# Hybrid decoder step: first norm's scale by quarters, conditioning loads by SyncE, last squares summed singly

## The chip, the cores and the metric

The kernel runs on 1 core of one Trainium2 chip. Its time is the device time of one execution in microseconds (us); a median of several runs is given where there are several. The engines are named as in the profile: PE (TensorE, matrix products), DVE (VectorE), ACT (ScalarE), POOL (GpSimd) and SP (SyncE, which here only issues DMAs). DMAs can be issued from SP, ACT and POOL, each with a queue of its own.

## The reference

One inference step of a decoder trunk with one layer, for a prompt of 256 tokens and 8 sample sequences of 4 tokens (288 columns in all), model width 2048, float32:

```python
mod = silu(c) @ w_ada + b_ada                      # c: one row for the prompt, one for each sample
sh1, sc1, gt1, sh2, sc2, gt2 = split(mod, 6)
xn = rmsnorm(x, g_norm1) * (1.0 + sc1) + sh1
proj = xn @ w_in                                   # LRU, GLA q k v, output gates, mLSTM, merge gates
merged = sum over 3 branches of sigmoid(gate_i) * (y_i @ w_br_i)
x = x + gt1 * (merged @ w_out)
xn = rmsnorm(x, g_norm2) * (1.0 + sc2) + sh2
x = x + gt2 * (square(relu(xn @ w_ff1)) @ w_ff2)
y = rmsnorm(x, g_final)
```

The three branches are an RG-LRU recurrence, gated linear attention and an mLSTM; the last two also read and write states of each sample sequence. Outputs are y and all new states.

## The kernel before

**Layout.** Activations lie with the 2048 features on the partitions, as 16 k-tiles of 128 x 288. Weights stream from memory in tiles of 0.5 MB (128 x 1024: two k-tiles by 512 output columns). Every product is made of float32r parts: a weight tile `raw` is split into `hi` (ACT, L156) and `lo` (DVE, L158), the activation into `xh` and `xl`, and PE adds hi*xh, hi*xl and lo*xh, 24 matmuls a weight tile (`stream`, L148 to L182). Three buffers each of `raw`, `hi` and `lo` let the loads run ahead of PE. SP issues the weight loads in the order in which the program is written (L68, a manual schedule for SP alone); the other engines' instructions are ordered by a scheduler.

**Conditioning.** `w_ada` is 6 kinds (SH1, SC1, GT1, SH2, SC2, GT2) of 2048 x 2048, loaded in units of 1 MB, 16 units a kind, multiplied on PE by silu(c) and put on the partitions by a transpose of `by_feature` (L229). `units()` (L344) lists all of them in order; `load_one()` issues the next unit's load, `visit()` runs the products of all units held, and after the last unit of a kind its `end` writes `mod`. A pattern given to `every()` (L187) says at which weight tile a load (L), a visit (V), a load of x (X) or a part of the norm's squares (N) is placed. `slots` names the buffers that the units take in turn: big tiles by number, `None` for the ring tile `ag`, `"st"` for two half tiles that the sample states also use. `slots["queue"]` is the engine that issues the load: SP at first, POOL from L588 on.

**The first norm.** The scale is applied to x before the first products (`scale`, L476); the row factor 1/rms is not known yet, so the first three blocks (q, k and a part of v, `NPRE = 3`) are multiplied by it afterwards (`by_rstd`, L520) and their shift is added as a product of its own (`shift_product`, L317). For the remaining blocks x is normalised and shifted in place (`normalise`, L498, `shift`, L505). Before, SC1 is made in two halves of 8 k-tiles: eight units and half of x come first, then the three blocks run over k-tiles 0 to 7 and, after the other half, over 8 to 15, added to the first pass on DVE (`add_slot`, L514).

**The sample states.** `mlstm()` (L1208) runs beside the output gate's streams; its state loads (`load`, L1393 to L1396) are issued by POOL into `st` and halves of slot 9, its stores by ACT.

**The end.** The last feed-forward product's evacuation (`ff2`, L1613) adds the residual and the squares of each k-tile (`sumsq`, L387): POOL sums the first 13, DVE adds tiles 13 and 14, and three matmuls with a matrix of ones sum over the partitions; `rstd_of` follows and the output is scaled and stored.

Of the kernel before, what the change touches and what calls it, by code (L numbers as in the profile page):

```python
# [52 lines left out]
def trunk(ctx, tc, io):  # L53
# [200 lines left out]
    def cond_product(name, load, each, cols, stat, finish):  # L254


        acc_ = []

        def products(raw, q):
            if not acc_:  # L260
                acc_.append(pa.tile([P, 512], F32, tag="pa", name=nm("pa")))
            ps = acc_[0]
            w = cols // len(raw)
            for i in range(each):
                k = each * q + i
                for h, r in enumerate(raw):
                    v = r[:, w * i:w * i + w].rearrange("p (m j f) -> p j m f", j=4, f=32)
                    for j in range(4):
                        pace["prod"] = T.matmul(ps[32 * j:32 * j + 32, h * w // 4:(h + 1) * w // 4], stat(k), v[:, j],  # L269
                                                start=k == 0 and h == 0, stop=k == KT - 1, skip_group_check=True)  # L270

        def end():
            hs = range(-(-cols // 1024))
            with tc.high_priority():
                pvs = [by_feature(acc_[0], h, min(256, cols // 4 - 256 * h)) for h in hs]
            for h in hs:
                with tc.high_priority():
                    finish(h, pvs[h])

        n = KT // each  # L280
        for q in range(n):
            def ld(q=q):
                raw = raw_tile()
                load(raw, q)
                return raw
            yield name, ld, lambda raw, q=q: products(raw, q), end if q == n - 1 else None

    def ada_finish(kind):
        def finish(h, pv):
            o = mod[:, kind, 8 * h:8 * h + 8, :]  # L290
            V.tensor_tensor(out=o, in0=pv[:, :, 0:9], in1=bada[:, kind, 8 * h:8 * h + 8].unsqueeze(2).to_broadcast([P, 8, 9]), op=ALU.add)
            if kind in (SC1, SC2):
                gg = Pm("g1" if kind == SC1 else "g2")
                V.scalar_tensor_tensor(o, o, 1.0, gg[:, 8 * h:8 * h + 8].unsqueeze(2).to_broadcast([P, 8, 9]), ALU.add, ALU.mult)
        return finish

    wada = io["wada"]

    def silu_c(k):
        return silc[:, 9 * k:9 * k + 32]  # L300
# [1 line left out]
    def ada(kind):  # L302
        def load(raw, k):
            if len(raw) == 2:
                for h in range(2):
                    slots["queue"].dma_start(raw[h], wada[kind, h, k])
            else:
                slots["queue"].dma_start(raw[0].rearrange("p (h m) -> p h m", h=2), wada[kind, :, k].rearrange("h p m -> p h m"))  # L308
        return cond_product(kind, load, 1, 2048, silu_c, ada_finish(kind))

    def ada_half(name, kind, h):

        def load(raw, q):
            slots["queue"].dma_start(raw[0].rearrange("p (k m) -> p k m", k=2), wada[kind, h, 2 * q:2 * q + 2].rearrange("k p m -> p k m"))
        return cond_product(name, load, 2, 1024, silu_c, lambda _, pv: ada_finish(kind)(h, pv))

    def shift_product(dst, nb):  # L317

# [23 lines left out]
    shifts = []  # L342

    def units():  # L344
        yield from ada_half("sc0", SC1, 0)
        yield from ada_half("sc", SC1, 1)
        yield from ada_half("sh0", SH1, 0)
        yield from ada_half("sh1", SH1, 1)
        yield from shift_product((qk, vv), NPRE)
        for k in (GT1, SH2, SC2, GT2):  # L350
            yield from ada(k)
# [9 lines left out]
    def visit(n=99):  # L361

        for _ in range(min(n, len(held))):
            name, raw, products, end = held.pop(0)
            products(raw)
            if end:
                end()
                done.add(name)

    def step(cs):  # L370
        for c in cs:
            if c == "L":
                load_one()
            elif c == "V":
                with tc.high_priority(), tc.issue_after(pace["last"].ins):
                    visit()
            elif c in also:
                also[c]()

# [22 lines left out]
            pace["sum"] = T.matmul(ps[:, :N], ones, sq, start=k == KT - 4, stop=k == KT - 1)  # L402

    pair = []

    def inv_sqrt(r, src, **ka):

# [48 lines left out]
    for u in range(8):  # L456
# [66 lines left out]
        yield  # L523

    def more_x():
        i = len(xs_)
        xs_.append(Q.dma_start(xb[:, 4 * i:4 * i + 4, :], io["x"][:, 8 + 4 * i:12 + 4 * i, :]))

    def norm_part():
        for k in range(4 * len(sums), 4 * len(sums) + 4):  # L530
            if k == 0:
                with tc.issue_after(pace["hi"].ins):
                    S.activation(ssq, xb[:, k, :], AF.Square)
                continue
            sq = t288()
            with tc.issue_after(pace["hi"].ins):
                S.activation(sq, xb[:, k, :], AF.Square)
            V.tensor_tensor(out=ssq, in0=ssq, in1=sq, op=ALU.add)
        sums.append(0)

    def second_half():
        while len(sums) < 2:
            yield
        with tc.issue_after(pace["last"].ins):
            T.matmul(ps[:, :N], ones, ssq, start=False, stop=True)
        inv_sqrt(rs, ps[:, :N], bias=eps, scale=1.0 / D)
        while "sc" not in done:
            yield
        for k in range(8, KT, 2):
            scale(k)  # L550
            yield
        for k in range(0, KT, 2):
# [8 lines left out]
    def last_shifts():  # L561
        for k in range(8, KT, 2):
            shift(k)
            if k != 8:
                yield

    xs_, sums = [], []
    ssq, rs = row("rr"), row("lf")
    also.update(X=more_x, N=norm_part)
    slots.update(ids=(2, 3, 4, 5, 6, 7, None), n=0)  # L570
    chain = {}
    with tc.high_priority():
        ready = scale(0, chain)
        for k in range(2, 8, 2):
            scale(k, chain)
    G.tensor_copy(con[:, 0:1], mod[:, SC1, 0, 0:1])
    G.dma_start(con, io["con"])
    every(". L X L LV LN XL LV LN LV L L L LV L L LLV L L L LV L L LLV")
    pre = beside(second_half())
    for h in range(2):  # L580
        for b in range(NPRE):
            ev = (add_slot if h else to_slot)((qk, vv)[b // 2], 4 * (b % 2))
            run(stream(win, B_Q + b, act1, 8 + 8 * h, ev, k0=8 * h, behind=None if h or b else ready))
            if h:
# [1028 lines left out]
    def ff2(hb, h):  # L1613
        for b in range(4):
            def ev(m, p, b=b):
                k = 4 * b + m
                a = facc[k // 8][:, k % 8, :]
                if hb == 0:
                    S.copy(a, p)
                    return  # L1620
                x = x2[k // 8][:, k % 8, :]
                if hb < 7:
                    V.tensor_tensor(out=a, in0=a, in1=p, op=ALU.add)  # L1623
                    if hb == 6:
# [147 lines left out]
```

## Time and profile before

| what | value |
|---|---|
| median of 3 runs (lowest to highest) | 1963.89 us (1963.37 to 1964.3) |
| profiled execution | 1962.52 us |
| its span | 1960.7 us |
| granted PE clock, mean | 0.995 |
| DMA moved | 429.01 MB, mean 219 GB/s |

The profile is of one execution. Its page gives busy shares by engine; a chain of waits follows the work that ended last back to what released it; other views list instructions in order of time, grouped by line, the waits of one engine, or the busy time of all engines in given stretches. Rows of the timeline have the start in us, the duration in us, engine, source line, operation, output <- input, and in brackets the idle time before it and what ended it. Rows of stretches give PE, PEld (weight loads into PE), DVE, ACT and POOL busy time with the instruction count, then the granted PE clock, the DMA share and GB/s.

### The profile page before, as it was taken

The page shows a single profiled execution, that of the slowest core. Times are in us where ns is not written, and L with a number is a line of the kernel's source. Part 1 is how long each engine was busy: PE and PEld are TensorE (multiplying, and loading weights), DVE is VectorE, ACT ScalarE, POOL GpSimd, SP SyncE. Part 2 cuts the span into 40 slices and gives each one's busy share as a digit, 9 for nine tenths or more (in the row PEclk, how much of TensorE's full clock was granted, in tenths as well). Part 3 has the DMA queues.
Part 4 walks back from the last instruction along what each step waited for, and adds up shares of the span by engine and source line. Part 5 has one row for each costly group of instructions (what it writes and reads, how often), then busy time and mean ns, then how long its engine had stood idle before and what let it go on. Part 6 is the DMA issues. An engine that isn't in the chain of part 4 may idle for free.

```text
span 1960.7 us, 35959 instructions
## 1 busy us (share of the span) xinstructions
PE 1921.1 (98%) x15060; PEld 1819.7 (93%) x15060; DVE 1028.6 (52%) x1567; ACT 823.7 (42%) x1179; POOL 267.2 (14%) x373
## 2 busy tenths in 40 slices
PE   7999999999999998999999999999999999999997
PEld 4889889999899997899998899999999999999997
DVE  2574746545683456654445564445444445444565
ACT  3433374544454343443333453443333334343433
POOL 0011200000132000012224431000000000010101
PEclk9999999999999999999999999999999999999999
DMA  9998766547744368957797555444444444444442
GB/s 385 408 381 301 262 243 239 199 151 262 267 149 145 136 205 296 310 215 272 276 360 280 190 187 204 169 159 169 169 163 160 172 162 162 162 168 170 164 172 106
DMA packets 116338, 429.01 MB, mean 219 GB/s; under 512 B 11776, under 2 KB 12064, under 8 KB 116048
## 3 DMA queue, kind: packets, MB, share of 16 engines
q1 hardware_dynamic: 85888, 313.26, 44.1%
q0 software_dynamic: 25536, 96.27, 13.4%
q10 hardware_dynamic: 4752, 17.19, 2.2%
q8 instruction: 118, 1.93, 0.4%
q14 instruction: 44, 0.36, 0.1%
HBM read 409.85 MB, written 16.81 MB: 218 GB/s over the span
## 4 chain that ended last, share of the span: by engine, by line
PE 93%; DMA 4%; DVE 2%; ACT 1%; issue 0%; DVEq 0%; SPq 0%; ACTq 0%; POOLq 0%
PE mm L165 83%; PE pa L269 4%; DMA raw<-win 2%; DMA st<-mC 1%; DMA raw<-wout 1%; DVE lo L158 1%; DMA s<-wada 0%; ACT hi L156 0%; PE px L677 0%; PE px L1429 0%; PE pi L1412 0%; PE px L948 0%; PE px L1343 0%; DVE s L597 0%; DMA o_C_s<-st 0%
## 5 line engine op out<-in xcount | busy, mean ns | idle before, releaser
L158 DVE TENSOR_TENSOR lo<-raw,hi 128x1024 fp32r<-128x1024 f32 x448 | 552.0, 1233 | 591.6 <-ACT hi L156 577.0
L156 ACT ACTIVATE hi<-raw 128x1024 fp32r<-128x1024 f32 x448 | 473.9, 1060 | 797.2 <-PE mm L165 656.8
L165 PE MATMUL mm<-xh,hi 128*128 128x288 f32 x2560 | 757.1, 300 | 2.9 <-ACT xh L493 1.8
L165 PE MATMUL mm<-xl,hi 128*128 128x288 f32 x2560 | 753.4, 297 | 0.0
L165 PE MATMUL mm<-xh,lo 128*128 128x288 f32 x2560 | 737.3, 296 | 1.6 <-DVE lo L158 1.6
L165 PE MATMUL mm<-s,hi 128*128 128x288 f32 x3328 | 659.5, 296 | 0.8 <-DVE rs_t L1545 0.8
L165 PEld LDWEIGHTS mm<-s,hi 128*128 128x128 f32 x3328 | 529.3, 188 | 6.3 <-issue 5.8
L165 PEld LDWEIGHTS mm<-xh,hi 128*128 128x128 f32 x2560 | 479.8, 188 | 21.8 <-issue 12.3
L165 PEld LDWEIGHTS mm<-xl,hi 128*128 128x128 f32 x2560 | 481.9, 188 | 2.7 <-issue 1.3
L165 PEld LDWEIGHTS mm<-xh,lo 128*128 128x128 f32 x2560 | 476.0, 188 | 4.2 <-DVE lo L158 2.7
L165 PE MATMUL mm<-s,lo 128*128 128x288 f32 x1664 | 477.3, 295 | 0.6 <-DVE lo L158 0.6
L165 PEld LDWEIGHTS mm<-s,lo 128*128 128x128 f32 x1664 | 308.6, 188 | 2.0 <-DVE lo L158 1.0
L158 DVE TENSOR_TENSOR lo<-s,hi 128x1024 fp32r<-128x1024 f32 x80 | 98.0, 1225 | 115.2 <-ACT hi L156 115.2
L1607 POOL TENSOR_TENSOR t<-t 128x288 f32<-128x288 f32 x64 | 60.2, 952 | 625.7 <-ACT t L1606 625.7
L156 ACT ACTIVATE hi<-s 128x1024 fp32r<-128x1024 f32 x80 | 84.9, 1061 | 143.2 <-PE mm L165 142.6
L1623 DVE TENSOR_TENSOR s<-s,mm 128x288 f32<-128x288 f32 x96 | 40.3, 450 | 33.9 <-PE mm L165 32.7
L269 PE MATMUL pa<-s,silc 128*32 128x256 f32 (+1 forms) x616 | 49.8, 450 | 5.5 <-DMA s<-wada 5.5
L269 PEld LDWEIGHTS pa<-s,silc 128*32 128x32 f32 x616 | 18.9, 112 | 25.5 <-issue 11.1
L429 DVE TENSOR_TENSOR s<-t,s 128x288 fp32r<-128x288 f32 x64 | 33.8, 568 | 15.5 <-ACT s L428 15.5
L308 POOL DMA_DIRECT2D ag<-wada x23 | 16.5, 719 | 169.7 <-PE pa L269 169.5
L428 ACT ACTIVATE s<-t 128x288 fp32r<-128x288 f32 x64 | 28.1, 443 | 24.6 <-POOL t L1607 24.6
L395 POOL TENSOR_TENSOR row<-row,t 128x288 f32<-128x288 f32 x24 | 22.4, 934 | 116.1 <-ACT t L393 115.1
(403 smaller groups left out, 1117.8 us busy)
## 6 DMA issues: line engine op xcount, KB each, us to landing
raw<-win SPq DMA_DIRECT2D x192, 512.0 KB, 4.4
raw<-wf SPq DMA_DIRECT2D x176, 512.0 KB, 4.1
s<-wf SPq DMA_DIRECT2D x80, 512.0 KB, 3.2
s<-wada SPq DMA_DIRECT2D x28, 1024.0 KB, 9.2
ag<-wada POOLq DMA_DIRECT2D x23, 1024.0 KB, 7.2
s<-wada POOLq DMA_DIRECT2D x21, 1024.0 KB, 10.9
raw<-wout SPq DMA_DIRECT2D x32, 512.0 KB, 4.7
st<-wada POOLq DMA_DIRECT2D x28, 512.0 KB, 8.0
```

Of the source, the lines that this page charges most:

```text
L156: pace["hi"] = S.activation(hi, raw, AF.Copy)
L158: pace["lo"] = V.tensor_tensor(out=lo, in0=raw, in1=hi.bitcast(F32), op=ALU.subtract)
L165: pace["last"] = T.matmul(ps, w[:, kk, ms], x, start=k == k0 and i == 0, stop=k == kt - 1 and i == 2)
L269: pace["prod"] = T.matmul(ps[32 * j:32 * j + 32, h * w // 4:(h + 1) * w // 4], stat(k), v[:, j], start=k == 0 and h == 0, stop=k == KT - 1 ...
L308: slots["queue"].dma_start(raw[0].rearrange("p (h m) -> p h m", h=2), wada[kind, :, k].rearrange("h p m -> p h m"))
L395: G.tensor_tensor(out=s, in0=s, in1=sq, op=ALU.add)
L428: S.activation(dst_h[:, r], src[:, r], AF.Copy)
L429: V.tensor_tensor(out=dst_l[:, r], in0=src[:, r], in1=dst_h[:, r].bitcast(F32), op=ALU.subtract)
L1607: G.tensor_tensor(out=r, in0=r, in1=r, op=ALU.mult)
L1623: V.tensor_tensor(out=a, in0=a, in1=p, op=ALU.add)
```

## The change

1. **Quarters.** SC1 is made in four quarters of 4 k-tiles, each of four 1 MB units from a copy of those weights laid out for it (`wsc`); the other kinds stay in `wada`. Before the first products four units and the first four k-tiles of x are loaded; the three blocks then run over k-tiles 0 to 3, 4 to 7 and 8 to 15, with two additions instead of one. The other quarters, the rest of x and the squares (all by `norm_part`, two k-tiles at a time) come in a new pattern, in which F visits at most four units. `normalise` and `shift` of k-tiles no longer end before the fourth block: they run beside it.
2. **SyncE.** From the output gate on (L1513) the conditioning loads are issued by SP instead of POOL. Patterns and buffers of those stages stay as they are.
3. **Last squares.** In the last feed-forward product POOL sums k-tiles 0 to 11; tiles 12 to 15 are not added to anything, and five matmuls with ones, placed behind the last weight product, sum them.

```diff
+                n = each // len(raw)
+                views = [raw[i // n][:, cols * (i % n):cols * (i % n) + cols]] if n else raw
+                w = cols // len(views)
...
-    def ada_finish(kind):
+    def ada_finish(kind, n=8):
         def finish(h, pv):
-            o = mod[:, kind, 8 * h:8 * h + 8, :]
...
+            r = slice(n * h, n * h + n)
+            o = mod[:, kind, r, :]
...
+    def ada_quarter(name, h):
+
+        def load(raw, q):
+            n = 2048 // len(raw)
+            for i, r in enumerate(raw):
+                Q.dma_start(r, io["wsc"][h, q, :, n * i:n * i + n])
+        return cond_product(name, load, 4, 512, silu_c, lambda _, pv: ada_finish(SC1, 4)(h, pv))
...
     def units():
-        yield from ada_half("sc0", SC1, 0)
-        yield from ada_half("sc", SC1, 1)
+        for h in range(4):
+            yield from ada_quarter(f"sc{h}", h)
...
-            elif c == "V":
+            elif c in "VF":
                 with tc.high_priority(), tc.issue_after(pace["last"].ins):
-                    visit()
+                    visit(4 if c == "F" else 99)
...
+    def sumsq_last(ps, x, k, s):
+
+        sq = s if k == 0 else t288()
+        pace["sq"] = S.activation(sq, x, AF.Square)
+        if 0 < k < KT - 4:
+            G.tensor_tensor(out=s, in0=s, in1=sq, op=ALU.add)
+        else:
+            pair.append(sq)
+        if k == KT - 1:
+            with tc.issue_after(pace["last"].ins):
+                for i, q in enumerate(pair):
+                    T.matmul(ps[:, :N], ones, q, start=i == 0, stop=i == 4)
...
     for i in range(2):
-        S.dma_start(xa[:, 4 * i:4 * i + 4, :], io["x"][:, 4 * i:4 * i + 4, :])
+        S.dma_start(xa[:, 2 * i:2 * i + 2, :], io["x"][:, 2 * i:2 * i + 2, :])
...
-    slots.update(ids=(2, 3, 4, 5, 6, 7, None, 9), n=0)
-    for u in range(8):
+    slots.update(ids=(2, 3, 4, 5, 6, 7, None, "st"), n=0)
+    for u in range(4):
         load_one()
...
-    def second_half():
-        while len(sums) < 2:
+    def next_scales():
+        for h in range(1, 4):
+            while f"sc{h}" not in done:
+                yield
+            for k in (4 * h, 4 * h + 2):
+                scale(k)
+                yield
+
+    def shifted():
+        while len(sums) < 6:
             yield
...
+        finish(scales)
+        for k in range(0, 12, 2):
             normalise(k)
             yield
...
-    every(". L X L LV LN XL LV LN LV L L L LV L L LLV L L L LV L L LLV")
-    pre = beside(second_half())
-    for h in range(2):
+    every("L L LX LN NV L LX LN LN FLX LL LN NFL L LL L FL L L FLL LL L FL LL")
+    scales = beside(next_scales())
+    beside(shifted())
+    for k0, k1 in ((0, 4), (4, 8), (8, KT)):
         for b in range(NPRE):
...
-    finish(pre)
-    every("L L L L . V")
-    slots.update(ids=(5, 6, 7, None, 0, 3), n=0, queue=G)
-    rest = beside(last_shifts())
+    every("L FL L L . V" + " L L L L . V" * 3)
+    slots.update(ids=(5, 3, 6, 7, None, 0), n=0, queue=G)
...
     merge(1, ygla, io["wbg"])
-    slots.update(ids=(None, 8), n=0)
+    slots.update(ids=(None, 8), n=0, queue=Q)
     every("L L . V" + 12 * " .", skip=11)
...
                 resid(x, p, GT2, k)
-                sumsq(pss, x, k, ssum)
+                sumsq_last(pss, x, k, ssum)
```

More of the change, by code (lines that the diff above doesn't have):

```diff
@@ L262, in products @@
             ps = acc_[0]
-            w = cols // len(raw)
             for i in range(each):
                 k = each * q + i
-                for h, r in enumerate(raw):
-                    v = r[:, w * i:w * i + w].rearrange("p (m j f) -> p j m f", j=4, f=32)
+                n = each // len(raw)
+                views = [raw[i // n][:, cols * (i % n):cols * (i % n) + cols]] if n else raw
+                w = cols // len(views)
+                for h, v in enumerate(views):
+                    v = v.rearrange("p (m j f) -> p j m f", j=4, f=32)
                     for j in range(4):
@@ L286, in cond_product @@
             yield name, ld, lambda raw, q=q: products(raw, q), end if q == n - 1 else None
-    def ada_finish(kind):
+    def ada_finish(kind, n=8):
         def finish(h, pv):
-            o = mod[:, kind, 8 * h:8 * h + 8, :]
-            V.tensor_tensor(out=o, in0=pv[:, :, 0:9], in1=bada[:, kind, 8 * h:8 * h + 8].unsqueeze(2).to_broadcast([P, 8, 9]), op=ALU.add)
+            r = slice(n * h, n * h + n)
+            o = mod[:, kind, r, :]
+            V.tensor_tensor(out=o, in0=pv[:, :, 0:9], in1=bada[:, kind, r].unsqueeze(2).to_broadcast([P, n, 9]), op=ALU.add)
             if kind in (SC1, SC2):
                 gg = Pm("g1" if kind == SC1 else "g2")
-                V.scalar_tensor_tensor(o, o, 1.0, gg[:, 8 * h:8 * h + 8].unsqueeze(2).to_broadcast([P, 8, 9]), ALU.add, ALU.mult)
+                V.scalar_tensor_tensor(o, o, 1.0, gg[:, r].unsqueeze(2).to_broadcast([P, n, 9]), ALU.add, ALU.mult)
         return finish
-    wada = io["wada"]
+    wada = {k: io["wada"][i] for i, k in enumerate((SH1, GT1, SH2, SC2, GT2))}
     def silu_c(k):
@@ L305, in load @@
                 for h in range(2):
-                    slots["queue"].dma_start(raw[h], wada[kind, h, k])
+                    slots["queue"].dma_start(raw[h], wada[kind][h, k])
             else:
-                slots["queue"].dma_start(raw[0].rearrange("p (h m) -> p h m", h=2), wada[kind, :, k].rearrange("h p m -> p h m"))
+                slots["queue"].dma_start(raw[0].rearrange("p (h m) -> p h m", h=2), wada[kind][:, k].rearrange("h p m -> p h m"))
         return cond_product(kind, load, 1, 2048, silu_c, ada_finish(kind))
@@ L313, in load @@
         def load(raw, q):
-            slots["queue"].dma_start(raw[0].rearrange("p (k m) -> p k m", k=2), wada[kind, h, 2 * q:2 * q + 2].rearrange("k p m -> p k m"))
+            for i, r in enumerate(raw):
+                n = 2 // len(raw)
+                a = 2 * q + n * i
+                slots["queue"].dma_start(r.rearrange("p (k m) -> p k m", k=n), wada[kind][h, a:a + n].rearrange("k p m -> p k m"))
         return cond_product(name, load, 2, 1024, silu_c, lambda _, pv: ada_finish(kind)(h, pv))
+    def ada_quarter(name, h):
+        def load(raw, q):
+            n = 2048 // len(raw)
+            for i, r in enumerate(raw):
+                Q.dma_start(r, io["wsc"][h, q, :, n * i:n * i + n])
+        return cond_product(name, load, 4, 512, silu_c, lambda _, pv: ada_finish(SC1, 4)(h, pv))
     def shift_product(dst, nb):
@@ L451, in to_slot @@
         return f
-    slots.update(ids=(2, 3, 4, 5, 6, 7, None, 9), n=0)
-    for u in range(8):
+    slots.update(ids=(2, 3, 4, 5, 6, 7, None, "st"), n=0)
+    for u in range(4):
         load_one()
-    for u in range(8):
+    for u in range(4):
         sq = t288()
@@ L525, in more_x @@
     def more_x():
-        i = len(xs_)
-        xs_.append(Q.dma_start(xb[:, 4 * i:4 * i + 4, :], io["x"][:, 8 + 4 * i:12 + 4 * i, :]))
+        k = 4 * len(xs_) + 4
+        xs_.append(Q.dma_start((xa, xb)[k // 8][:, k % 8:k % 8 + 4, :], io["x"][:, k:k + 4, :]))
     def norm_part():
[L530 to L535, printed above, removed]
+        for k in range(2 * len(sums) + 4, 2 * len(sums) + 6):
+            sq = ssq if k == 4 else t288()
             with tc.issue_after(pace["hi"].ins):
-                S.activation(sq, xb[:, k, :], AF.Square)
-            V.tensor_tensor(out=ssq, in0=ssq, in1=sq, op=ALU.add)
+                S.activation(sq, xin(k), AF.Square)
+            if k > 4:
+                V.tensor_tensor(out=ssq, in0=ssq, in1=sq, op=ALU.add)
         sums.append(0)
-    def second_half():
-        while len(sums) < 2:
+    def next_scales():
[7 more added lines that the diff above has]
+        while len(sums) < 6:
             yield
@@ L546, in second_half @@
         inv_sqrt(rs, ps[:, :N], bias=eps, scale=1.0 / D)
[L547 to L552, printed above, removed]
+        finish(scales)
+        for k in range(0, 12, 2):
             normalise(k)
@@ L559, in second_half @@
             yield
-    def last_shifts():
+        for k in range(12, KT, 2):
+            normalise(k)
+            yield
+        while "sh1" not in done:
+            yield
         for k in range(8, KT, 2):
             shift(k)
-            if k != 8:
-                yield
+            yield
     xs_, sums = [], []
@@ L569, in trunk @@
     also.update(X=more_x, N=norm_part)
-    slots.update(ids=(2, 3, 4, 5, 6, 7, None), n=0)
     chain = {}
@@ L573, in trunk @@
         ready = scale(0, chain)
-        for k in range(2, 8, 2):
-            scale(k, chain)
+        scale(2, chain)
     G.tensor_copy(con[:, 0:1], mod[:, SC1, 0, 0:1])
     G.dma_start(con, io["con"])
-    every(". L X L LV LN XL LV LN LV L L L LV L L LLV L L L LV L L LLV")
-    pre = beside(second_half())
-    for h in range(2):
+    every("L L LX LN NV L LX LN LN FLX LL LN NFL L LL L FL L L FLL LL L FL LL")
+    scales = beside(next_scales())
+    beside(shifted())
+    for k0, k1 in ((0, 4), (4, 8), (8, KT)):
         for b in range(NPRE):
-            ev = (add_slot if h else to_slot)((qk, vv)[b // 2], 4 * (b % 2))
-            run(stream(win, B_Q + b, act1, 8 + 8 * h, ev, k0=8 * h, behind=None if h or b else ready))
-            if h:
+            ev = (add_slot if k0 else to_slot)((qk, vv)[b // 2], 4 * (b % 2))
+            run(stream(win, B_Q + b, act1, k1, ev, k0=k0, behind=None if k0 or b else ready))
+            if k1 == KT:
                 beside(by_rstd((qk, vv)[b // 2], 4 * (b % 2)))
-    finish(pre)
-    every("L L L L . V")
-    slots.update(ids=(5, 6, 7, None, 0, 3), n=0, queue=G)
-    rest = beside(last_shifts())
+    every("L FL L L . V" + " L L L L . V" * 3)
+    slots.update(ids=(5, 3, 6, 7, None, 0), n=0, queue=G)
     for b in range(NPRE, 4):
@@ L1735 @@
         "x": np.ascontiguousarray(fm(x)), "ct": np.ascontiguousarray(fm(c)), "par": np.ascontiguousarray(par), "con": _consts(),
-        "wada": np.ascontiguousarray(I["w_ada"][0].reshape(KT, P, 6, 2, 1024).transpose(2, 3, 0, 1, 4)), "win": pack(win), "wsm": np.ascontiguousarray(wsm.reshape(KT, P, 32).transpose(1, 0, 2)).reshape(P, 512),
+        "wada": np.ascontiguousarray(I["w_ada"][0].reshape(KT, P, 6, 2, 1024)[:, :, [SH1, GT1, SH2, SC2, GT2]].transpose(2, 3, 0, 1, 4)),
+        "wsc": np.ascontiguousarray(I["w_ada"][0].reshape(4, 4, P, 6, 4, 512)[:, :, :, SC1].transpose(3, 0, 2, 1, 4)).reshape(4, 4, P, 2048), "win": pack(win), "wsm": np.ascontiguousarray(wsm.reshape(KT, P, 32).transpose(1, 0, 2)).reshape(P, 512),
         "lruw": np.ascontiguousarray(np.concatenate([I["lru_w_a"][0], I["lru_w_x"][0]], 0).transpose(1, 0, 2)).reshape(P, 2048),
```

## The prediction

> **What bounds the kernel now.** I read the page first, then what the matmul engine waited for, then the chain of waits over the first 140 us, then the stretches where a wait stands. The page's shares of busy time and its row of DMA slices:
>
> ```profile
> PE 1921.1 (98%) x15060; PEld 1819.7 (93%) x15060; DVE 1028.6 (52%) x1567; ACT 823.7 (42%) x1179; POOL 267.2 (14%) x373
> DMA  9998766547744368957797555444444444444442
> ```
>
> PE is the bound nearly everywhere, so only time in which PE stands still, or works before its real work can begin, is to be had. The DMA row says where else to look: its first three slices (147 us) are full. PE's waits hold two that the change touches, and the chain of waits shows a third loss that the list hides, the start (start us, us, what):
>
> ```profile
> PE pi L1412 <- DMA st<-mC: 7.6, 1, 7.6
> PE pi L402 <- POOL row L395: 1.2, 1, 1.2
> ...
> 9.87 19.68 DMA raw<-win
> ...
> 29.58 1.06 ACT hi L156
> ...
> 31.19 17.66 PE mm L165 x120
> 87.27 3.59 PE pa L269 x64
> 104.82 9.76 PE mm L165 x72
> ```
>
> The first weight product of the projections starts at 31.19. From there a streamed weight tile (24 matmuls) costs PE 9.76 / 3 = 3.25 us, and a batch of four conditioning units (64 matmuls) 3.59 us.
>
> **First norm by quarters.** The timeline of the start: the fourth and the eighth conditioning unit, the first tile's low part, the fourth weight load, the first matmul of the second tile, and the last products of the stage; then two stretches with their DMA rate (last column GB/s).
>
> ```profile
> 17.38 1.07 PE L269 MATMUL pa<-s,silc 128*32 128x256 f32 x16 [0.29 <-DMA s<-wada]
> 28.37 1.07 PE L269 MATMUL pa<-s,silc 128*32 128x256 f32 x16 [0.69 <-DMA s<-wada]
> 32.02 1.22 DVE L158 TENSOR_TENSOR lo<-raw,hi 128x1024 fp32r<-128x1024 f32 x1
> 33.31 0.33 SPq L155 DMA_DIRECT2D raw<-win  x1
> 35.98 0.29 PE L165 MATMUL mm<-xh,hi 128*128 128x288 f32 x1
> 132.79 2.77 PE L269 MATMUL pa<-s,silc 128*32 128x256 f32 x48
> 0.00:20.00 20.00, 10.32 (x78) 4.16 (x82) 0.75 (x5) 4.71 (x10) 1.40 (x8) 1.00 0.92 363
> 40.00:50.00 10.00, 10.00 (x91) 9.41 (x94) 3.88 (x5) 5.05 (x10) 0.00 (x0) 1.00 1.02 409
> ```
>
> Before, eight units of 1.05 MB must arrive ahead of the first scaled tile; the last lands at 28.37 and PE starts 2.82 us later. After, four units do. The fourth landed at 17.38 with 5.73 MB moved (four units, 1.18 MB of x, 0.35 MB of small tables); with half of x not yet asked for it is 5.14 MB, so 15.6 us by proportion, and the start is 15.6 + 2.8 = 18.4. That is 12.8 us earlier. The first weight tile lands just behind the last unit in both (chain: 9.87 + 19.68 = 29.55).
>
> Not all of it stays. The number of units until the end of the shift is the same 32, so four of them, which ran while PE had nothing else, now run in the PE-bound stretch: one batch, +3.6. Next, what is late: SyncE's order after the change is four units, tile 0, unit, tile 1, unit, tile 2, unit, x, tile 3, unit, tile 4. Tile 3 waits for the low part of tile 0 (rows: 33.24 against a start at 31.19, so 2.1 after it, 20.5), when 7.3 MB are delivered by the first row's rate; up to its end 11.3 MB are asked for, so at 0.41 MB/us it lands at 29.8 and its two parts are made by 32.1 (1.06 + 1.22). PE gets there at 18.4 + 4.8 (first tile, 31.19 to 35.98) + 2 x 3.25 = 29.7: a wait of 2.4. Tile 4 lands one unit and one tile (1.57 MB, 3.8 us) later, ready at 35.9, while PE is free at 35.4: 0.5. Together +2.9. After that PE is the slower side: six tiles and one batch take 23.1 us of PE and bring 3.1 + 4.2 + 1.2 MB, 20.7 us of DMA; the later twelve tiles with their four batches take 53.4 us and bring 23 MB, 56 us, which eats 3 us of the 6 to 8 us by which the units then lead. Ends for this wait: 0 (weights arriving beside, not behind, the units) and +6 (the lead is gone).
>
> VectorE gets work: a third pass over the accumulated blocks, and four more squares to add. The groups by line over 31 to 140 us:
>
> ```profile
> L517 DVE TENSOR_TENSOR s<-s,mm 128x288 f32<-128x288 f32 x12 | 5.4, 454 | 13.5 <-PE mm L165 13.0
> L538 DVE TENSOR_TENSOR row<-row,t 128x288 f32<-128x288 f32 x7 | 3.2, 457 | 0.9 <-DVE row L538 0.5
> ```
>
> Twelve more of the first (5.4 us), four more of the second (1.8 us) and two more ends of a product are 9 us of VectorE in a stretch of some 100 us. The low part of the weights, which PE needs, queues behind them on VectorE. It is hidden by the three buffers of low parts as long as VectorE does not run in bursts of more than two tiles; if the cover goes, each block's edge costs about a tile's low part, 1.2 us, at three edges: ends 0 and +4, value +1. In the stretch of before, 31.19 to 135.56 (132.79 + 2.77), 24 tiles (78.0) and 24 units (21.5) leave 4.9 us of losses: I leave them as they are, at best half of them go (-2.4).
>
> Start: -12.8 + 3.6 + 2.9 + 1.0 = **-5.3**, ends -11.6 and +0.8. The longer conditioning stage is otherwise the same afterwards: the 16 shift units keep GpSimd's queue and the same visits per tile.
>
> The rate row above is 409 GB/s, held over 10 us; 49 MB (32 units, 24 tiles, x and tables) at that rate are in by 120 us. The Trainium skill, "DMA: Bandwidth & Descriptors", Specifications, gives about 358 GB/s as the share of HBM of one core; by it the 49 MB would need 137 us, as long as the stage takes now, and the start would be worth nothing. By that figure the trace disagrees, with one core running, and the row decides.
>
> **Conditioning loads by SyncE.** GpSimd's DMA issues, PE's steps at the sample state, the issue table's median for the state loads, the weight loads' landing times between 752 and 776 us, three stretches' rows and the chain's row of the products that use the loads:
>
> ```profile
> 755.91 0.71 POOL L308 DMA_DIRECT2D s<-wada  x1
> 756.62 0.72 POOL L308 DMA_DIRECT2D ag<-wada  x1
> 758.37 0.56 POOL L1396 DMA_DIRECT2D st<-mC  x1 [1.03 <-DMA o_C_s<-st]
> 775.07 1.08 PE L1412 MATMUL pi<-st,s 128*32 128x257 f32 x8 [7.62 <-DMA st<-mC]
> 787.36 0.64 PE L1412 MATMUL pi<-s,s 128*32 128x257 f32 x8
> st<-mC POOLq DMA_DIRECT2D x8, 514.0 KB, 5.9
> DMA to landing us min/median/max: 5.2/9.8/10.8
> 768.00:775.00 7.00, 0.00 (x0) 0.00 (x0) 0.00 (x0) 2.59 (x5) 1.07 (x2) 0.79 1.03 413
> 775.00:785.00 10.00, 9.93 (x67) 9.12 (x68) 6.03 (x12) 1.87 (x2) 0.00 (x0) 0.81 0.47 150
> 824.65 1.85 PE pa L269 x16
> ```
>
> The two conditioning loads of the output gate go into GpSimd's queue long before they are needed (products at 824.65) and 2 us ahead of a state load that is needed at 767.4. That load lands 16.7 us after issue instead of 5.9, and PE stands 7.6 us; then its granted clock is 0.81 for 10 us, up to 1.9 us more, of which I count 1.5 (the same eight matmuls take 1.08 against 0.64). In SyncE's order, written by hand, the two loads stand behind weight tiles 11 and 12 of the gate, and SyncE issues weight tiles some five ahead of PE, so about nine tiles before their visit: by 824.65 - 9 less 9 x 3.25, before 786, and some 15 us behind this state load. It then lands at 758.4 + 6 = 764.4, 3 us before use. Next late are the following state loads, which now share the wires with the two units but not the queue: in the crowded stretch above the weight loads, of the same size on their own queue, took at most 10.8 us, and the state loads are issued about 10 us ahead of use. I leave 0.6 for that. State loads: -7.6 - 1.5 + 0.6 = **-8.5**, ends -9.1 and -4 (half a new wait).
>
> The Trainium skill, "DMA: Bandwidth & Descriptors", Issuing engines are not separate DMA queues, says otherwise: loads from GpSimd, SyncE and ScalarE run on the same 16 engines and interleave, and another issuer saves only its issue time. By that alone this term would be zero; it is a rival below. The 10.8 against 16.7 us speaks against it.
>
> At the output projection GpSimd again issues a burst, eight units between these rows (first and last), and weight tiles come late on the chain of waits; PE's waits of 980 to 1060 us:
>
> ```profile
> 987.16 1.44 POOL L308 DMA_DIRECT2D xl<-wada  x2 [18.43 <-PE mm L165]
> 1003.30 1.46 POOL L308 DMA_DIRECT2D s<-wada  x2
> 1010.21 9.43 DMA raw<-wout
> 1022.09 6.48 DMA raw<-wout
> PE mm L165 <- DVE rs_t L1545: 0.8, 1, 0.8
> PE mm L165 <- DVE lo L158: 0.6, 1, 0.6
> ```
>
> SyncE spreads them, one between two weight tiles: 1.57 MB per 3.25 us for six tiles is 3.8 us of DMA each, a debt of 3.5 us against the tiles' lead. **-1.2**, ends -1.4 and +1.5. GpSimd loses 40 units' issues of 0.7 to 1.1 us; at 14% busy that is worth nothing.
>
> **Last squares singly.** The timeline of the end:
>
> ```profile
> 1946.74 0.75 PE L402 MATMUL pi<-row,ones 128*128 128x288 f32 x2 [1.18 <-POOL row L395]
> 1946.83 0.78 ACT L393 ACTIVATE t<-s 128x288 f32<-128x288 f32 x2 [0.58 <-DVE s L1547]
> 1947.82 1.24 PE L402 MATMUL pi<-t,ones 128*128 128x288 f32 x4 [0.33 <-DVE t L400]
> ```
>
> GpSimd's last addition and VectorE's pair sum leave the path. Two more sums are added (0.62 each, 1.24 / 2), but three of the five can run before the last two squares, which exist at about 1947.3 and 1947.6. From 1947.3 two sums end at 1948.5, against 1949.06: **-0.5**, ends -0.8 and +0.4 (all five behind one another, late).
>
> **The sum.** -5.3 - 8.5 - 1.2 - 0.5 = -15.5. The profiled execution took 1962.5 (span 1960.7 and 1.8 around it): 1947.0. The median of the runs shown, 1963.89, is 1.4 above it: **1948.4**.
>
> **Rivals.** The rows for the third (what SyncE waited for; the landing of units on SyncE's queue):
>
> ```profile
> SPq L155 <- DVE lo L158: 1431.9, 389, 11.1
> s<-wada SPq DMA_DIRECT2D x28, 1024.0 KB, 9.2
> ```
>
> First: the start stays with the DMA. The full slices speak for it: 49 MB must land by the end of the shift whenever PE begins. Then PE begins early and stands later, the start term is about -1, and the time 1952.7. Against it: from 40 to 50 us PE was full (row above) while 409 GB/s came in, and the tally of tile and unit bytes against PE's time leaves a lead.
>
> Second: another queue does not help the state load. The wires are full (413 GB/s, 1.03) and the two units, wherever issued, delay one state load by the same wait. Terms -5.3, -1.2, -0.5: 1955.5 + 1.4 = 1956.9 if it stays whole. (This is the Trainium skill's rule on issuing engines, cited above.) Against it: in SyncE's order the units come some 15 to 25 us later, at another state load, and the weight loads of that stretch fared better on a queue of their own.
>
> Third, slower: SyncE stands. A unit waits for its buffer until PE has used the unit before it, and the weight tiles queue behind that wait; they feed ScalarE and VectorE and through these PE. In the third branch a buffer is freed four tiles before the next visit, so a tile behind it has about 13 us of lead less 2.3 for its two parts. A unit's 9.2 and then a tile's share of 1.3 make 10.5, just below. If the pair takes over 11, each of eight such places costs up to one tile: 8 x 3.25 = +26, with the other terms -15.5 it is 1974. Against it: SyncE's 1431.9 us of waits are waits for free buffers, so its loads are ahead.
>
> **Chances.** What a measurement here tells from no change is about 0.2% (4 us). Forecast 0.63, first rival 0.16, second 0.11, third 0.08, and 0.02 that the scheduler's new order gives back all. Forecast, first and second lie below 1960 but for their edges: faster 0.86, same 0.06, slower 0.08. The range takes the good ends of the start (-11.6 in place of -5.3) on one side, 1942, and the second rival with its edge on the other, 1958. The third stays outside.
>
> **What would show it.** First projection matmul at 18 to 19 us; waits of PE for low parts of 2 to 4 us in 28 to 36; the last shift batch some 5 us earlier; no row of PE waiting for the state load, and clock 1.00 there; all conditioning loads after the output gate on SyncE with no idle on PE behind them; five sums together at the end. Wrong if the first matmul starts after 22, if PE's weight waits add up to over 10 us, or if the state row stands.

## The result and the profile after

The changed kernel takes 1946.99 us (median of 4, 1946.26 to 1947.35) beside 1963.63 on the same chip (median of 4). The ratio is 0.9917 (95% interval 0.99 to 0.9934): 16.6 us less. The forecast was 1948.4, range 1942 to 1958. The profiled execution has a span of 1945.5, 15.2 below that of before.

The page after, its engine shares, and three of PE's waits:

```profile
PE 1917.2 (99%) x15312; PEld 1823.5 (94%) x15312; DVE 1035.3 (53%) x1588; ACT 823.6 (42%) x1179; POOL 237.3 (12%) x322
PE mm L165 <- ACT hi L156: 3.6, 5, 1.5
PE mm L165 <- DVE lo L158: 2.5, 4, 0.7
PE pi L1439 <- DMA s<-mC: 0.6, 1, 0.6
```

The 7.6 us wait for a state load is 0.6, the wait for POOL's last sum is gone, and among PE's waits for weights the one for the high parts of weight tiles, 0.2 before, now stands first. Where the time came from is read by laying the chains of both kernels beside each other at the same pieces of work. Before, the first shift products, the third branch's last visit and the output projection's first visit (start us, us, what):

```profile
155.50 2.72 PE pa L269 x32
991.76 2.72 PE pa L269 x32
1049.50 3.58 PE pa L269 x40
```

After, the same three, and the output gate's visit (824.65 before) as the second row:

```profile
152.72 2.72 PE pa L271 x32
812.44 1.85 PE pa L271 x16
979.78 2.72 PE pa L271 x32
1035.36 3.58 PE pa L271 x40
```

The lead is 2.8 us after the start stage (2.6 us ahead of the sample states: 730.35 against 727.74 for the same products), 12.2 after the states, 12.0 at the third branch's end, 14.1 at the output projection. So the start gave 2.8, the states 9.6 and the output projection 2.2. The end adds 0.8: from the last residual to the transpose of the sums it is 1945.73 to 1949.17 before and 1931.78 to 1934.38 after.

The start after, first PE's timeline and then SyncE's (the weight tiles `raw` and where units `wsc` stand between them):

```profile
15.54 1.08 PE L271 MATMUL pa<-s,silc 128*32 128x128 f32 x32 [0.20 <-DMA s<-wsc]
18.27 1.33 PE L165 MATMUL mm<-xh,hi 128*128 128x288 f32 x8 [1.64 <-ACT xh L520]
22.58 0.40 PE L165 MATMUL mm<-xh,hi 128*128 128x288 f32 x1 [0.87 <-ACT hi L156]
27.14 0.40 PE L165 MATMUL mm<-xh,hi 128*128 128x288 f32 x1 [0.92 <-ACT hi L156]
32.25 0.40 PE L165 MATMUL mm<-xh,hi 128*128 128x288 f32 x1 [1.47 <-ACT hi L156]
36.89 0.40 PE L165 MATMUL mm<-xh,hi 128*128 128x288 f32 x1 [0.42 <-ACT s L477]
```

```profile
3.35 0.44 SPq L155 DMA_DIRECT2D raw<-win  x1
4.25 0.33 SPq L328 DMA_DIRECT2D s<-wsc  x1
4.63 0.47 SPq L155 DMA_DIRECT2D raw<-win  x1
9.18 0.33 SPq L328 DMA_DIRECT2D s<-wsc  x1
9.55 0.43 SPq L155 DMA_DIRECT2D raw<-win  x1
```

The first matmul of the projections is 12.9 us earlier (31.19 to 18.27), and then each of the next three tiles begins late; the fourth stops after its first two matmuls, for ScalarE's copy of a finished block (L477). From the first matmul to the first visit (40.84) PE takes 22.6 us; before, it took 17.7 (31.19 to 48.86). The two stretches do not hold quite the same work: PE's timeline has 120 matmuls of weight tiles in it before (five tiles) and 126 after, since six of the sixth tile run ahead of the visit. At 3.25 us for 24 these six are 0.8 us, so the five tiles themselves take 21.8 and the loss is 4.1 us.

The states after: SyncE's issues of the gate's two units, landing times of the state loads issued between 745 and 770 us, and the stretch in which PE stood before:

```profile
778.06 0.38 SPq L311 DMA_DIRECT2D ag<-wada  x1
784.58 0.41 SPq L311 DMA_DIRECT2D s<-wada  x1
DMA to landing us min/median/max: 6.0/8.0/8.6
770.00:780.00 10.00, 9.44 (x79) 8.38 (x78) 6.45 (x13) 4.09 (x7) 1.06 (x2) 1.00 0.98 333
```

### The profile page after: what moved, and what is told of

Read it like the earlier page. It is cut to its first block, busy times and chain, and to the rows that moved or that the text cites. A ratio compares the mean times of both kernels' runs of the same rounds, so it can differ in the third digit from the quotient of the medians.

```text
span 1945.5 us, 36472 instructions
## 1 busy us (share of the span) xinstructions
PE 1917.2 (99%) x15312; PEld 1823.5 (94%) x15312; DVE 1035.3 (53%) x1588; ACT 823.6 (42%) x1179; POOL 237.3 (12%) x322
## 4 chain that ended last, share of the span: by engine, by line
PE 94%; DMA 2%; DVE 2%; ACT 1%; issue 0%; DVEq 0%; SPq 0%; ACTq 0%; POOLq 0%
PE mm L165 84%; PE pa L271 5%; DMA raw<-win 1%; DVE lo L158 1%; DMA s<-mC 0%; ACT hi L156 0%; PE px L704 0%; PE px L1456 0%; PE px L975 0%; PE px L1370 0%; PE pi L1439 0%; DMA o_C_s<-s 0%; DVE s L624 0%; PE px L1380 0%; PE pi L993 0%
## 5 line engine op out<-in xcount | busy, mean ns | idle before, releaser
L271 PE MATMUL pa<-s,silc 128*32 128x128 f32 (+2 forms) x744 | 46.0, 386 | 2.1 <-DMA s<-wsc 2.1
L1137 POOL TENSOR_TENSOR s<-s,t 128x288 f32<-128x288 f32 x16 | 21.0, 1336 | 178.5 <-DVE t L1136 178.5
L271 PEld LDWEIGHTS pa<-s,silc 128*32 128x32 f32 x744 | 22.2, 115 | 16.6 <-issue 9.5
L271 PE MATMUL pa<-ag,silc 128*32 128x512 f32 (+2 forms) x280 | 28.6, 502 | 0.0
```

Of the source, the lines that this page charges most:

```text
L1137: (V if br == 1 else G).tensor_tensor(out=a, in0=a, in1=t, op=ALU.add)
```

## The experiments

Times are medians; a ratio is to the kernel before on the same chip. First each part by itself and one order of the start (e1 to e4), then the mechanisms (e5 to e9 and e12), then two kernels again side by side.

**e1, SyncE alone.**

```diff
-    slots.update(ids=(None, 8), n=0)
+    slots.update(ids=(None, 8), n=0, queue=Q)
     every("L L . V" + 12 * " .", skip=11)
```

> The kernel before with one edit: conditioning loads from the output gate on are issued by SyncE. From the two traces of before and after, milestones of PE moved by 9.6 us over the sample states and by 2.2 us at the output projection. Theory (the parts stand for themselves): 1963.6 - 11.8, about 1951.8; no row of PE waiting for the state load longer than 1 us. Rival A (the new queue makes no difference, the states came through because everything before them moved): within 3 us of 1963.6 and the 7.6 us wait stands. Rival B (part of it is SyncE's order at the output projection alone): about 1961.

Measured: 1950.22 against 1962.74, ratio 0.9935 (0.992 to 0.9949). The chain:

```profile
814.60 1.85 PE pa L269 x16
981.76 2.72 PE pa L269 x32
1037.34 3.58 PE pa L269 x40
```

The gate's visit is 10.1 us earlier than before though nothing ahead of the gate changed, and the way from the second row to the third is 55.6 us against 57.7. PE has no wait for a state load among its rows. Rivals A and B fall. The edit moves the two units to another queue and also to a later moment (SyncE issues them at 780.9 and 786.6 us, GpSimd issued them at 755.9 and 756.6); e5 and e12 try to part the two.

**e2, quarters alone.** The kernel after with `queue=Q` taken out at that place and `sumsq` put back.

> The kernel after with GpSimd's queue and the old sum of the last squares put back: only the quarters are changed. Theory: the start's milestone, 2.8 us, is all that is left, 1960.9, and the 7.6 us wait for the state load is back. Rival (the early start also moved the states' loads apart): 1953 or less, the wait gone or halved.

Measured: 1958.69, ratio 0.9981 (0.9971 to 0.9991); span 1958.0, 2.7 below before. The wait is back:

```profile
PE pi L1439 <- DMA st<-mC: 7.2, 1, 7.2
```

**e3, last squares alone.** `sumsq_last` in the kernel before.

> The kernel before with the new sum of the last squares alone. Theory: 0.8 us between the last residual and the transpose of the row sums, 1962.8; inside what the times can tell, so the interval from the last product's first residual to the transpose decides: 3.4 us before (1945.73 to 1949.17), 2.6 expected. Rival (the gain came from another order of VectorE at the end): 3.2 or more.

Measured: 1961.79, ratio 0.9996 (0.9987 to 1.0005): the times can't tell it. The last residual and the transpose stand at 1946.45 and 1949.05, 2.60 us apart where it was 3.44. The three parts alone sum to 12.5 + 4.05 + 0.95 = 17.5 us of medians, and together they gave 16.6.

**e4, weights first.**

```diff
-    every("L L LX LN NV L LX LN LN FLX LL LN NFL L LL L FL L L FLL LL L FL LL")
+    every(". . LX LN LLNV L LX LN LN FLX LL LN NFL L LL L FL L L FLL LL L FL LL")
```

> The kernel after with the second quarter's four units moved behind the weight tiles in SyncE's order: none behind tiles 0 and 1, one each behind tiles 2 and 3, two behind tile 4 ahead of the visit. Same loads, same bytes by the visit. Theory (the first five tiles, 22.6 us where 17.7 were taken before, wait for weights queued behind units): these five take 17.5 to 19.5 us, time 1943 to 1945. Rival A (VectorE's and ScalarE's additional work, the third pass and the squares, makes the tiles late): no change, 1946.5 to 1947.5. Rival B (the bytes are the bound): what the tiles gain the visit loses, it starts 3 us or more after the tile ahead of it, 1946 to 1948.

Measured: 1944.46 (1944.04 to 1949.04), ratio 0.9911 (0.9896 to 0.9926). First matmul and first visit:

```profile
18.29 1.29 PE L165 MATMUL mm<-xh,hi 128*128 128x288 f32 x8 [1.54 <-DVE xh L500]
36.65 1.96 PE L271 MATMUL pa<-s,silc 128*32 128x128 f32 x64
```

These five tiles take 18.4 us (120 matmuls, as before), and in the kernel after 21.8: 3.4 of the 4.1 us that the start lost there came from units ahead of weight tiles in one queue. (The expectation took 22.6, with the six matmuls of the sixth tile.) Rival A falls for this stretch. Rival B holds in part: see e11.

**e5 and e12, the gate's units early, on SyncE.** The kernel after, with

```diff
-    every("L L . V" + 12 * " .", skip=11)
+    every("L L . . . . . . . V" + 12 * " .", skip=5)
```

> The kernel after with the output gate's two conditioning loads placed six weight tiles earlier in SyncE's order (behind tiles 5 and 6; the visit stays behind tile 14's place less one), so that they are issued near 750 to 760 us, beside the same state loads as before, but on SyncE's queue. Theory (what delayed the state load was 2 MB ahead of it in its own queue): the state loads land in 11 us at most, PE waits for them 2 us at most, time 1946.5 to 1948.5. Rival (any 2 MB on the wires at that moment delays it; the later moment is what helped): PE waits 5 us or more and runs at a lower clock after it, 1953 to 1957.

> e5 again, for a second profile: in e5 the profiled execution took 1948.05 with 0.5 us of waiting for the state load, the timed ones about 1952. Theory (the queue decides, the margin is thin: the state loads landed in 9.5 us where 10 were to be had): an execution of 1952 shows a wait of 3 to 4 us for a state load or for its store, and one of 1948 none. Rival (the timed ones lose elsewhere): an execution of 1952 with less than 1 us of such waits.

Measured: e5 1952.13 (1948.05 to 1953.68), ratio 0.9942 (0.9927 to 0.9957); e12 1950.17 (1949.83 to 1951.76), 0.9939 (0.9923 to 0.9956). The profiled execution of e5 took 1948.05, that of e12 1950.49. SyncE's issues, PE's wait, the state load that it waits for (start of its way, us on the way) and the stretch, e5:

```profile
755.24 0.38 SPq L311 DMA_DIRECT2D ag<-wada  x1
759.25 0.59 SPq L311 DMA_DIRECT2D s<-wada  x1
PE pi L1439 <- DMA st<-mC: 0.5, 1, 0.5
755.44 9.21 DMA st<-mC
760.00:770.00 10.00, 9.52 (x96) 8.71 (x95) 6.85 (x19) 4.41 (x9) 0.53 (x1) 1.00 1.03 391
```

and e12:

```profile
PE pi L1439 <- DMA st<-mC: 2.0, 1, 2.0
756.18 9.56 DMA st<-mC
760.00:770.00 10.00, 8.03 (x73) 6.91 (x72) 5.25 (x15) 4.11 (x8) 0.53 (x1) 0.83 1.03 387
```

The first unit is issued within about 1 us of where POOL issued it before (755.91 there), on wires as full (1.03), and the state load lands in 9.2 and 9.6 us where it took 16.7. The queue shows in the order of landing: in e5 the load goes out 0.2 us behind the first unit and lands at 764.65, while neither unit landed before 766.9 (in e12 it goes out 1.3 us behind the unit and lands 1.4 behind it); before, the two units and the load behind them landed in the order of their issue, at 767.7, 773.4 and 775.0. But these runs are not the same case as before in every respect. Here the state load itself goes out 2 to 3 us earlier, and the second unit 3.8 us (e5) and 2.7 us (e12) behind it, where both units were ahead of it before. So they show that a unit on another queue holds the load up little; how much of the 7 us two units ahead of it on another queue would cost is not shown. The later moment helps too: here PE waits 0.5 to 2.0, and after the longer wait its clock is lower, while the kernel after, on another chip, is 3.2 to 5.1 us faster than e12 and e5. The gate's visit starts at 813.46 in e5's profile and 815.90 in e12's; that 2.4 is the difference of the two profiled executions. Executions of 1952 to 1954 were not profiled, so what they lose beyond e12's 2.0 us wait stays open.

**e6, output projection by GpSimd.**

```diff
-    slots.update(ids=(None, "st", 8, 9, "xh", ...), n=0)
+    slots.update(ids=(None, "st", 8, 9, "xh", ...), n=0, queue=G)
```

> The kernel after with GpSimd's queue put back from the output projection on (gate and third branch stay on SyncE). Theory (GpSimd issues eight units within some 16 us as soon as buffers are free, and the weight tiles come late): the two long weight waits on the chain return, PE's stretch from the last visit of the third branch to the first of the output projection goes from 55.6 to 57.7 us, 1949. Rival (the 2.2 us came from another order of the engines there): no change, 1947.

Measured: 1948.45, ratio 0.9926 (0.991 to 0.9943), 1.5 above the kernel after.

```profile
980.05 2.72 PE pa L271 x32
1037.66 3.58 PE pa L271 x40
```

57.6 us again, as forecast: GpSimd's burst costs 2.0 us of PE's time there by this profile and 1.5 by the medians.

**e7, three passes alone.** The kernel before with the loop

```diff
-    for h in range(2):
+    for k0, k1 in ((0, 4), (4, 8), (8, KT)):
```

> The kernel before with its first three blocks in three passes (k-tiles 0 to 3, 4 to 7, 8 to 15) and all else unchanged: eight units first, two halves of the scale. It has the additions on VectorE and the block edges of the change, and none of its early start. Theory (the third pass costs PE about 0.6 us at each of three more edges): the stage's last products end 1 to 3 us later than 135.6, time 1964 to 1965.5. Rival (the pass is hidden; the early start loses to the weights' order alone): 135.6 within 0.5, 1962.7.

Measured: 1961.85, ratio 0.9997 (0.9987 to 1.0006). The last products of the stage:

```profile
131.99 3.63 PE pa L269 x64
```

They end at 135.6, as before. The third pass, its twelve additions on VectorE and its block edges cost nothing measurable when nothing else is changed. The theory in its expectation falls.

**e8, squares later.** e4 with the last N two tiles later (`FL L LLN` for `NFL L LL`).

> The kernel with the weights first (e4), and the last part of the squares two weight tiles later, so that the root, the normalising of x and the last quarter's scale do not meet on VectorE. In e4 PE takes 15.5 us for the four tiles between the third quarter's products and the first shift products, 13.0 would be enough. Theory (VectorE's burst there puts the low parts late): that stretch falls to 13.5 to 14.5, time 1943.0 to 1944. Rival (it is the scale's own way from the visit to the next tile): 15.5 stays, 1944.5.

Measured: 1944.55, ratio 0.9911 (0.9897 to 0.9924). The third quarter's and the first shift products in e8, then the same in e11 (which is e4 again):

```profile
73.18 3.63 PE pa L271 x128
93.15 3.59 PE pa L271 x64
```

```profile
73.91 3.67 PE pa L271 x128
93.06 3.59 PE pa L271 x64
```

Between them lie 16.3 and 15.5 us. The theory falls: taking the root out of the way of the scale does not shorten the stretch.

**e9, no units at the gate.** The kernel before with `every("")` in the gate's place.

> The kernel before without the output gate's two conditioning loads at that place; they come later, with the third branch's, still by GpSimd. Theory (these two units alone delay the state load): PE's 7.6 us wait and the low clock after it are gone, 1953 to 1955. Rival (the state load is late for its own store and the crowd of stores): the wait stays at 4 us or more, 1959 or more.

Measured: 1956.7, ratio 0.9972 (0.9961 to 0.9984): neither forecast. GpSimd's issues and PE's wait show why:

```profile
755.31 0.71 POOL L308 DMA_DIRECT2D ag<-wada  x1 [0.77 <-DVE s L1110]
758.51 0.55 POOL L1396 DMA_DIRECT2D st<-mC  x1 [2.49 <-DMA o_C_s<-st]
PE pi L1412 <- DMA st<-mC: 3.0, 1, 3.0
DMA to landing us min/median/max: 5.0/6.2/11.1
```

A unit of the next stage, whose buffer was free, went out at the same moment in their place. It makes a better experiment than the one meant: with two units ahead in GpSimd's queue the state load lands in 16.7 us and PE waits 7.6 (e2: 7.2), with one in 11.1 and 3.0, with one beside and one behind it on SyncE's queue in 9.2 to 9.6 and 0.5 to 2.0, and with none near (after) in 8.6 at most and 0.6.

**e10 and e11, the kernel after and e4 again.**

> The kernel after again, to compare with e8 and e11 on one chip: 1946 to 1947.5.

> e4 again on the same chip as the kernel after: 2 to 3 us below it by every theory that holds so far; within 0.5 if e4's gain was the chip's.

Measured: 1946.74 and 1944.81, ratios 0.9922 (0.9909 to 0.9934) and 0.9911 (0.9898 to 0.9925). The intervals overlap; all four runs of e11 (1944.69 to 1945.41) lie below all five of e10 (1946.09 to 1947.93), and e4's median lay 2.5 below that of after. With e8, which differs from it by less than the runs can tell, it is the fastest version here. First and second visit, e10 and then e11:

```profile
40.84 3.63 PE pa L271 x128
60.39 3.67 PE pa L271 x128
```

```profile
37.37 3.67 PE pa L271 x128
58.97 3.67 PE pa L271 x128
```

Of 3.5 us gained at the first visit 1.4 is left at the second. For 0.8 of the difference there is a plain reason: e10 has 126 matmuls of weight tiles ahead of its first visit and e11 120, and at the second both have 240. On e4's chain between the two stand the next quarter's scale and the high parts behind it on ScalarE, then a low part behind the evacuations on VectorE:

```profile
41.23 0.96 ACT xh L520 x3
43.23 0.97 ACT hi L156
51.48 1.23 DVE lo L158
```

That they cost the other 1.3 us is a reading that was not tried by an experiment.

## Why the prediction was right, and where it was not

The time came within 1.4 us of the forecast by luck: two errors met. The start gave 2.5 us less than forecast, and the three other terms gave 2.4 more. The mechanism of each term held in the main, but none of the sizes did, and in the start the wait also began earlier and at another part than forecast.

**Start: -5.3 forecast, -2.8 measured.** The first matmul came at 18.27, forecast 18.4. The step that failed is the wait for weights, 2.9 forecast and 4.1 measured (21.8 us against 17.7): the tally of bytes in SyncE's order was set against PE's need from tile 3 on, and tiles 1 and 2 were taken as in time because before they had landed long before PE began. With the start 12.9 us earlier they had not: PE's rows show waits at 22.58 and 27.14 already, and like that of tile 3 at 32.25 they are for the high part (ScalarE, first to need the landed tile), not the low part as forecast. By the text's own rule tile 1 lands after 7.2 MB, at 20 us, with its parts made by 22.3, 0.9 us ahead of the forecast end of the first tile, and tile 2 has 0.3 us. Margins that small should have stood in the tally: tile 1 landed at 21.45 (the chain: issued 4.63, 16.82 on the way), and the first tile was done in 3.4 us instead of the 4.8 taken from before, when the granted clock was 0.83 over 30 to 40 us (1.00 in the first tile after). So the first tile gained 1.4 us and the four behind it lost 5.5. Two slips in the tally for tile 3 nearly cancel: its own list sums to 11.0 MB, not 11.3, and 4.0 MB from 20.5 us at 0.41 MB/us land at 30.3, not 29.8; put right, the wait comes to 2.6 instead of 2.9. e4 shows the cause for 3.4 of the 4.1. The VectorE term, +1.0, is zero for the third pass by itself (e7). In all, 6.7 us more than before's losses were lost in the stage (first matmul to the same products, less 3.6 for the four units: 18.27 to 139.77 against 31.19 to 142.4); 4.1 are in the first five tiles, and 2.6 are spread behind them. Their cause stays open: not the pass alone, not the root and the normalising (e8).

The rival that the start stays with the DMA was half right: the gain is nearer to its -1 than to -5.3. In the first five tiles it was not the bytes to the end of the shift that held PE but the order of the first 11 MB. The Trainium skill's figure of 358 GB/s ("DMA: Bandwidth & Descriptors", Specifications) is exceeded here, with one core running: after the change 50 to 60 us ran at 424 GB/s.

**States: -8.5 forecast, -9.6 measured.** The wait went from 7.6 to 0.6 and the clock after it is 1.00 (row 770 to 780). The loads were issued at 778 and 785, forecast before 786; the state loads landed in 8.6 us at most, the weight loads' 10.8 having been the bound. The 0.6 left for a new wait is what came, but for a load that went out at 767.65, before the units, so they did not cause it. The wait (7.0) and the clock (up to 1.9) make 8.9 of the 9.6; the rest was not traced.

**Output projection: -1.2 forecast, -2.2 measured,** and e6 gives it back. PE's rows of waits, 0.8 and 0.6, were taken as the whole price; weight loads into PE, which have rows of their own, waited there too (1.0 us for low parts before, none after), and that is the likely rest; e6 does not part it.

**End: -0.5 forecast, -0.8 measured** (e3: 3.44 to 2.60). Beyond the sums, the last squares themselves came 0.3 us sooner: they are done at 1933.32 after, against 1947.61 before less the lead of 13.95 at the last residual.

**The rivals.** That another queue makes no difference fell with e5 and e12: with one unit issued beside the state load and one behind it on SyncE's queue, on full wires, the load lands in 9.2 to 9.6 us, 0.6 to 1.0 us above the slowest state load of the kernel after, where two ahead in its own queue made it 16.7. Two units ahead of it on another queue were not run. The Trainium skill says both things on one page ("DMA: Bandwidth & Descriptors"): under "Issuing engines are not separate DMA queues" that another issuer saves only its issue time, which e5 speaks against (a load issued behind a unit on another queue landed ahead of it), and under "Queues, rings and completion order" that each DMA engine goes round its queues, which agrees with 9.2 us against 16.7 as far as these runs go. That SyncE stands on buffers did not happen: no wait of PE behind a conditioning load appears from the gate on.

## What to carry to other kernels

Two loads in one queue landed in the order of their issue here (before, the units at 767.7 and 773.4, the state load at 775.0), so a load that is needed soon must not stand behind one that is needed late: taking 2 MB from in front of a load, by another queue and a later moment, took away 7 us of waiting at one place, and putting four units behind the weight tiles gave 2 us at another. When a start is pulled forward, tally the bytes of the queue, in its order, against the need of every consumer from the first on, because loads that used to be early have lost their lead. The removed burst was worth more (2.2 us) than PE's waits listed for it (1.4), and an experiment that takes a load away must be read in the trace for what the scheduler put in its place.

## What the runs showed of the hardware

A wait of PE of 2.0 us (e12) was followed by a mean granted clock of 0.83 over the 10 us stretch around it, one of 0.5 us (e5) by 1.00; before, 7.6 us of waiting had a row of 0.81. In rows of 1 us, e12's clock is 0.50 from 766 to 769 us, just behind the wait. So a wait a quarter as long cost about the same in clock, some 1.7 us of 10. That was not expected: the forecast counted the clock only with the whole wait. Nor does the length of the wait settle it, for e9's wait of 3.0 us, between the two, cost nothing in clock. It lies in this row, and the next 10 us have 1.00 too:

```profile
765.00:775.00 10.00, 6.95 (x76) 6.14 (x76) 4.95 (x14) 4.21 (x8) 1.06 (x2) 1.00 0.92 346
```

What decides between the 2.0 us of e12 and the 3.0 us of e9 is not shown. The Trainium skill, "TensorE: Matmul & The Clock Gate", Part 1, has the clock halved after an idle window of about 3.4 us. That e9's wait left the clock whole agrees with it; in e12's profile 2.0 us of waiting sufficed, which does not, if the wait's row is the whole of the idle time.
